# Last feed-forward chunk of a hybrid decoder layer: one bank state added from PSUM, and the closing LayerNorm's statistics, by VectorE; the scaling by ScalarE

## The chip, the cores and the metric

The kernel runs on one core of one Trainium2 chip. The metric is the device time of one execution in microseconds (us). The time before is the median of three runs, 904.08 us, between 903.46 and 904.77.

## The reference, cut to what matters

The layer is: a LayerNorm, a token mixer (gated linear attention and multi-head latent attention in parallel, gated and projected), a LayerNorm over the sum with the residual, a squared-ReLU feed-forward net, and the closing LayerNorm (LN2). All is float32, with 512 tokens and 1024 channels. What matters here is the end:

```
def layer_norm(x, g, b):
    mu = jnp.mean(xf, axis=-1, keepdims=True)
    var = jnp.mean(jnp.square(xf - mu), axis=-1, keepdims=True)
    return ((xf - mu) * lax.rsqrt(var + LN_EPS) * g + b).astype(x.dtype)
...
ff = jnp.square(jax.nn.relu(h @ w_ff1[l])) @ w_ff2[l]        # 512x1024 @ 1024x4096, @ 4096x1024
h = layer_norm(DEEPNORM_ALPHA * h + ff, ln2_g[l], ln2_b[l])
```

## The kernel before, in words

The 512 tokens are four tiles of 128 tokens (`tt` 0 to 3). `res[tt]` is a 128 x 1024 tile in SBUF with the residual (alpha times h, with LN1's weight and bias in it); the feed-forward result is added into it. Every float32 product is made of three matmuls over operands that are split into a high and a low part (`split`, lines 106 and 107, and `pump`, lines 180 and 181: ScalarE makes the high part, VectorE the low part).

The 4096 hidden channels are worked through in four chunks of 1024 (`ci` 0 to 3). In each chunk `gemm_fm` makes the hidden activations, and `win_f2` the second product, in Winograd's form of Strassen's scheme: seven block products ("phases" 0 to 6) over sums of token blocks, channel blocks and weight blocks. A phase has two halves, each one entry of the list `WIN`, and works on two token sub-tiles `t`. Phases 0, 3 and 6 accumulate in the same PSUM bank for each `t`, and so do phases 2 and 5; phase 1 and phase 4 have banks of their own. After the second half of a phase the bank's state is read out (lines 1160 to 1165): ScalarE copies it from PSUM into a tile `ev` (line 1163), and a DMA issued by GpSimd (POOL) adds it in SBUF to the halves of `res` that need it (line 1165). Columns 0 to 511 of a tile are its half `j` = 0, columns 512 to 1023 its half `j` = 1.

The last chunk (`end`) goes through the first eight entries (phases 0 to 3) in this way. The fourth state is that of phase 3: it is added to half 1 of tiles 0 and 1. The other three phases are then worked one sub-tile at a time by `tile_product`, and VectorE adds the bank straight to `res`: phase 5 to half 1 of tiles 0 and 1 (line 1182), phase 6 to both halves of tiles 2 and 3 (line 1189), phase 4 taken off half 0 of tile 2 (line 1192) and, in two pieces of 256 columns, of tile 3 (line 1200).

When a tile has its last term, `ln2(tt)` normalises it. Before the change there are three forms:

- Tile 0: VectorE makes the statistics (`bn_stats` on each half, line 1048, `bn_aggr`, line 1049), ScalarE adds epsilon and turns the mean's sign (lines 1050 and 1051).
- Tiles 1 and 2: ScalarE makes them, in two passes over 1024 columns that also give a sum (lines 1055 and 1056), and a small third instruction (line 1057).
- For tiles 0 to 2 POOL raises the variance to the power of -0.5 (line 1058), ScalarE makes `nmr` = -mean times that (line 1059) and normalises the tile (line 1060), VectorE multiplies by LN2's weight `gb[0]` (line 1061), and POOL issues a DMA that adds the tile to the output rows in DRAM (line 1062). Those rows were filled with LN2's bias beforehand by SyncE's (SP's) DMAs (line 1158).
- Tile 3: VectorE makes the statistics in four pieces of 256 columns (lines 1196 and 1201) and joins them (line 1065); epsilon (line 1066), POOL's power (line 1067), then VectorE subtracts the mean and multiplies by the weight in two halves (line 1070), multiplies by the power and adds the bias in two halves (line 1073), and SP stores each half (line 1074).

The order of the work in each engine's queue is set ahead of time by a planner with a cost model of its own; each queue then runs in that order, and an instruction that waits holds all behind it. `tc.issue_after(x)` keeps an instruction behind `x` in the planned order.

Of the kernel before, what the change touches and what calls it, by code (L numbers as in the profile page):

```python
# [10 lines left out]
F32 = mybir.dt.float32  # L11
# [4 lines left out]
AF = mybir.ActivationFunctionType  # L16
ALU = mybir.AluOpType
AX = mybir.AxisListType

P = 128  # L20
T = 512
D = 1024
NT = T // P
NK = D // P
LN_EPS = 1e-5
# [27 lines left out]
def tile_hybrid_block(ctx: ExitStack, tc: tile.TileContext, I, out, dbg=None):  # L53
    nc = tc.nc
# [10 lines left out]
    def nm(s):  # L65
        uid[0] += 1
        return f"{s}_{uid[0]}"
# [4 lines left out]
    def A(shape, dt=F32, n="a"):  # L72
        tag, bufs = ("C", 8) if n in TAG_C else (n, TAG_W[n]) if n in TAG_W else ("A", 24)
        return pa.tile(shape, dt, tag=tag, bufs=bufs, name=nm(n))

    def B(shape, dt=F32, n="b"):
        return pb.tile(shape, dt, tag="B", name=nm(n))

    def S(shape, dt=F32, n="s"):
        return sm.tile(shape, dt, tag=n, name=nm(n))  # L80
# [4 lines left out]
    def PX(shape=(P, T), dt=F32, n="px"):  # L85
        return px.tile(list(shape), dt, tag="px", name=nm(n))
# [4 lines left out]
    act = nc.scalar.activation  # L91
    vtt = nc.vector.tensor_tensor
    vts = nc.vector.tensor_scalar
    stt = nc.vector.scalar_tensor_tensor
    gtt = nc.gpsimd.tensor_tensor
    mm = nc.tensor.matmul

    def bcast_row(name):
        t = A([P, D], F32, "bc")
        src = I[name]  # L100
        nc.scalar.dma_start(t, bass.AP(tensor=src.tensor, offset=src.offset, ap=[[0, P], [1, D]]))
        return t
# [24 lines left out]
    mhalf = consts.tile([P, 8], F32, name="mhalf")  # L127
# [7 lines left out]
    st = {"dma": 0, "spl": 0, "gates": ()}  # L135
# [60 lines left out]
    def spawn(g):  # L196
        active.append(g)
        return g

    def step(g):  # L200
        try:
            next(g)
        except StopIteration:
            active.remove(g)
# [3 lines left out]
    def tick(width):  # L208
        for g in list(active[:width or WID[0]]):
            step(g)  # L210

    def finish(*gs):
        while any(g in active for g in gs):
            for g in list(active):
                if g in gs:
                    step(g)
# [113 lines left out]
    def win_items(ci):  # L330
        return WIN if ci < FC - 1 else WIN[:8] + WIN[10:12] + WIN[8:10] + WIN[12:]
# [421 lines left out]
    scale = HQ ** -0.5  # L753
# [205 lines left out]
    t0, mv = mla_pair(0)  # L959
    mv()  # L960
    y_gla(1)
    t1, mv = mla_pair(1)
    mv(lambda: finish(*t0))
    t2, mv = mla_pair(2)
    mv(lambda: finish(*t1))
    t3, mv = mla_pair(3)
    mv(lambda: finish(*t2))
    y_mla(0)
    res = []
# [66 lines left out]
            yield  # L1036


    def ln2(tt, bst=None):
        r = res[tt]  # L1040
        rows = out[tt * P:(tt + 1) * P, :]
        if tt < 3:
            mv, nmr = S([P, 2], F32, "mv"), S([P, 1], F32, "nmr")
            nmean, var = mv[:, 0:1], mv[:, 1:2]
            if tt == 0:
                bst = S([P, 2, 6], F32, "bst")
                for j in range(2):
                    nc.vector.bn_stats(bst[:, j, :], r[:, j * T:(j + 1) * T])
                nc.vector.bn_aggr(mv, bst)
                act(var, var, AF.Copy, bias=LN_EPS)  # L1050
                act(nmean, nmean, AF.Copy, scale=-1.0)
            else:

                j = A([P, D], F32, "junk")
                act(j, r, AF.Copy, scale=-1.0 / D, accum_out=nmean)
                act(j, r, AF.Square, bias=nmean, accum_out=var)
                act(var, var, AF.Copy, scale=1.0 / D, bias=LN_EPS)
            gtt(var, var, mhalf[:, 0:1], op=ALU.pow)
            act(nmr, nmean, AF.Copy, scale=var)
            act(r, r, AF.Identity, scale=var, bias=nmr)  # L1060
            vtt(r, r, gb[0], op=ALU.mult)
            nc.gpsimd.dma_start(rows, r, accum_op=ALU.add)
        else:
            mv = S([P, 2], F32, "mv")
            nc.vector.bn_aggr(mv, bst)
            vts(mv[:, 1:2], mv[:, 1:2], LN_EPS, None, op0=ALU.add)
            gtt(mv[:, 1:2], mv[:, 1:2], mhalf[:, 0:1], op=ALU.pow)
            for j in range(2):
                c = slice(j * T, (j + 1) * T)
                stt(r[:, c], r[:, c], mv[:, 0:1], gb[0][:, c], op0=ALU.subtract, op1=ALU.mult)  # L1070
            for j in range(2):
                c = slice(j * T, (j + 1) * T)
                stt(r[:, c], r[:, c], mv[:, 1:2], gb[1][:, c], op0=ALU.mult, op1=ALU.add)
                nc.sync.dma_start(rows[:, c], r[:, c])
        yield

    def win_load(ci):
        w2 = I["w_ff2"].rearrange("(k p) n -> p k n", p=P)
# [43 lines left out]
    def win_f2(ci, hid):  # L1122
        bank = {}
        end = ci == FC - 1
        items = win_items(ci)

        def product(n, pp, t, cols=slice(0, T), new=None):
            op, hf, ph = items[n]
            hi, lo = stream[PL["f2", ci][n]]["w"]
            key = ({3: 0, 6: 0, 5: 2}.get(ph, ph), t)  # L1130
            opens = key not in bank
            if opens:
                bank[key] = (PX if key[0] < 2 else MM)()
            o, c = bank[key], slice(t * P, (t + 1) * P)
            if new is not None:
                o, opens = new, hf == 0 and pp == 0
            while ph not in hid[2 * hf + pp]:
                tick(4)
            xh, xl = hid[2 * hf + pp][ph]
            mm(o, xh[:, c], hi[:, pp, cols], start=opens, stop=False, skip_group_check=True)  # L1140
            mm(o, xh[:, c], lo[:, pp, cols], start=False, stop=False, skip_group_check=True)  # L1141
            mm(o, xl[:, c], hi[:, pp, cols], start=False, stop=hf == 1 and pp == 1, skip_group_check=True)  # L1142
            return o

        for n, (op, hf, ph) in enumerate(items[:8] if end else items):
            pump(PL["f2", ci][n])
            for pp in range(2):
                for t in range(2):
                    product(n, pp, t)
                tick(4)  # L1150
            if n in (5, 6):
                t2, q21 = WT.pop((ci, n - 5))
                vtt(t2, t2, q21, op=ALU.subtract)
                WQ[ci, "T4", n - 5] = t2
            if end and n == 6:
                gb.extend([bcast_row("ln2_g"), bcast_row("ln2_b")])
                for tt in range(3):
                    nc.sync.dma_start(out[tt * P:(tt + 1) * P, :], gb[1])
            if hf == 1:
                for t in range(2):  # L1160
                    o = bank[{3: 0, 6: 0, 5: 2}.get(ph, ph), t]
                    e = B([P, T], F32, "ev")
                    st["ev"] = act(e, o, AF.Copy, scale=-1.0 if ph == 4 else 1.0)  # L1163
                    for tt, j in (((0, 0),), ((0, 0),), ((2, 1),), ((0, 1),), ((2, 0),), ((0, 1),), ((2, 0), (2, 1)))[ph]:
                        nc.gpsimd.dma_start(res[tt + t][:, j * T:(j + 1) * T], e, accum_op=ALU.add)  # L1165
            if n == 9 and not end:
                win_load(ci + 1)
        if not end:
            return

        pump(PL["f2", ci][13])

        def tile_product(ns, t, c0=0, w=T, new=None):
            for n in ns:
                for pp in range(2):
                    o = product(n, pp, t, slice(c0, c0 + w), new)
                    tick(4)
            return o

        for t in range(2):  # L1180
            o = tile_product((8, 9), t)
            vtt(res[t][:, T:], res[t][:, T:], o, op=ALU.add)
            spawn(ln2(t))
        bst = S([P, 4, 6], F32, "bst4")
        for t in range(2):
            r = res[2 + t]
            o = tile_product((12, 13), t)
            r2 = r.rearrange("p (j c) -> p j c", c=T)
            vtt(r2, r2, o[:, None, :].to_broadcast([P, 2, T]), op=ALU.add)
            if t == 0:  # L1190
                o = tile_product((10, 11), t)
                vtt(r[:, :T], r[:, :T], o, op=ALU.subtract)
                spawn(ln2(2))
                continue
            for j in range(2):
                nc.vector.bn_stats(bst[:, 2 + j, :], r[:, T + j * 256:T + (j + 1) * 256])
            for j in range(2):
                c = slice(j * 256, (j + 1) * 256)
                o = tile_product((10, 11), t, j * 256, 256, PX()[:, :256])
                vtt(r[:, c], r[:, c], o, op=ALU.subtract)  # L1200
                nc.vector.bn_stats(bst[:, j, :], r[:, c])
        finish(spawn(ln2(3, bst)))

    gb = []
    WQ, WT = {}, {}
# [81 lines left out]
```

## Time and profile before

| What | Value |
|---|---|
| median of three runs | 904.08 us (903.46 to 904.77) |
| profiled execution: span from the first to the last instruction | 901.4 us |
| mean granted TensorE clock of the span | 0.995 |
| TensorE matmul busy | 878.1 us, 97% of the span |
| VectorE busy | 566.1 us, 63% |
| ScalarE busy | 439.8 us, 49% |
| GpSimd busy | 172.8 us, 19% |

The page gives the span of the profiled execution and no time of its own beside that. The span is 2.7 us under the median of the runs; a difference between two spans is therefore read as the same difference between two times. In the rows PE is TensorE (matmuls), DVE is VectorE, ACT is ScalarE, POOL is GpSimd and SP is SyncE. A row of a timeline has the start in us from the span's start, the duration in us, the engine, the line of the kernel, the operation, and output<-input; brackets tell how long the engine had been idle before it and what released it. Successive instructions of one engine overlap by a little, so that starts lie closer together than durations. Rows with x2 cover two instructions. Matmul ends are modelled.

### The profile page before, as it was taken

Reading aid. Unit: us, or ns where it says so; the run is one execution under the profiler, and the core shown is the slowest. Engines: PE = TensorE matmul, PEld = TensorE weight load, DVE = VectorE, ACT = ScalarE, POOL = GpSimd, SP = SyncE. Lnnn points to the kernel's source line nnn. Section 1 sums busy time; section 2 is a strip of 40 time slices with the busy share of each in tenths; the row PEclk is TensorE's granted clock in tenths of the full one; section 3 lists DMA queues with packets and bytes.
Section 4 is the critical chain, followed back from the end, with each engine's and each line's share of the span. In section 5 each row is a group of like instructions: output and inputs, shape, how many; then the busy total and the mean of one; then the engine's idle time right before and its main releaser. Section 6 shows DMA issues by size and latency. Waiting matters only on the chain.

```text
span 901.4 us, 11728 instructions
## 1 busy us (share of the span) xinstructions
PE 878.1 (97%) x4472; PEld 746.5 (83%) x4472; DVE 566.1 (63%) x919; ACT 439.8 (49%) x745; POOL 172.8 (19%) x203
## 2 busy tenths in 40 slices
PE   5999999999999999999999999999999999999994
PEld 5988888888888888888888888988888888888883
DVE  7835855575635244657756797997557656754666
ACT  5555443444434333435645423366357546645654
POOL 1003442442511010000000002104400520241032
PEclk9999999999999999999999999999999999999997
DMA  7413213212213332212207618005940990397084
GB/s 243 122 47 94 90 52 94 71 47 71 75 38 93 88 105 74 68 42 65 94 24 260 205 49 303 2 0 139 302 120 25 261 249 25 80 312 169 1 210 94
DMA packets 63335, 101.47 MB, mean 113 GB/s; under 512 B 7680, under 2 KB 31616, under 8 KB 63280
## 3 DMA queue, kind: packets, MB, share of 16 engines
q1 hardware_dynamic: 48256, 64.04, 22.7%
q0 software_dynamic: 13104, 33.04, 15.2%
q10 hardware_dynamic: 1920, 3.66, 1.2%
q8 instruction: 35, 0.57, 0.3%
q14 instruction: 20, 0.16, 0.1%
HBM read 82.36 MB, written 3.67 MB: 95 GB/s over the span
## 4 chain that ended last, share of the span: by engine, by line
PE 92%; DMA 2%; ACT 2%; POOL 1%; issue 1%; DVE 1%; POOLq 0%; DVEq 0%; ACTq 0%
PE mm L231 16%; PE mm L233 15%; PE mm L232 15%; PE mm L264 6%; PE mm L265 6%; PE mm L266 6%; PE px L1141 3%; PE px L1140 3%; PE px L1142 3%; PE mm L1141 2%; PE mm L1140 2%; PE mm L1142 2%; PE px L680 2%; DMA res<-ev 1%; PE px L837 1%
## 5 line engine op out<-in xcount | busy, mean ns | idle before, releaser
L181 DVE TENSOR_TENSOR wlo<-wraw,whi 128x1024 fp32r<-128x1024 f32 (+1 forms) x104 | 117.7, 1132 | 162.3 <-ACT whi L180 154.9
L231 PE MATMUL mm<-h,whi 128*128 128x512 f32 x416 | 162.6, 392 | 0.4 <-ACT gt L924 0.4
L232 PE MATMUL mm<-h,whi 128*128 128x512 f32 x416 | 162.4, 390 | 0.0
L180 ACT ACTIVATE whi<-wraw 128x1024 fp32r<-128x1024 f32 (+1 forms) x104 | 100.3, 964 | 118.7 <-PE mm L232 68.3
L233 PE MATMUL mm<-h,wlo 128*128 128x512 f32 x416 | 154.9, 390 | 0.0
L1165 POOL DMA_DIRECT2D res<-ev x56 | 48.6, 980 | 238.2 <-ACT ev L1163 195.8
L231 PEld LDWEIGHTS mm<-h,whi 128*128 128x128 f32 x416 | 78.1, 188 | 16.3 <-ACT gt L924 0.6
L233 PEld LDWEIGHTS mm<-h,wlo 128*128 128x128 f32 x416 | 77.9, 188 | 16.4 <-DVE wlo L181 0.3
L232 PEld LDWEIGHTS mm<-h,whi 128*128 128x128 f32 x416 | 78.2, 188 | 15.6
L265 PE MATMUL mm<-wlo,h 128*128 128x512 f32 x128 | 50.3, 393 | 0.0
L266 PE MATMUL mm<-whi,h 128*128 128x512 f32 x128 | 50.1, 392 | 0.0
L264 PE MATMUL mm<-whi,h 128*128 128x512 f32 x128 | 49.7, 403 | 0.0
L1214 ACT ACTIVATE relu<-mm 128x512 f32<-128x512 f32 x32 | 18.8, 595 | 56.8 <-PE mm L233 56.8
L352 POOL TENSOR_TENSOR mv<-mv,mhalf 128x1 f32<-128x1 f32 x4 | 4.6, 1154 | 211.7 <-DVE mv L351 211.7
L619 POOL TENSOR_TENSOR rp<-rp 128x256 f32<-128x256 f32 x32 | 31.4, 983 | 60.9 <-ACT E L624 44.1
L626 DVE TENSOR_TENSOR M<-E,qk 128x512 f32<-128x512 f32 x32 | 27.3, 853 | 16.5 <-ACT E L624 16.5
L624 ACT ACTIVATE E<-rp 128x512 f32<-128x512 f32 x32 | 20.4, 638 | 26.9 <-POOL rp L620 26.9
L180 ACT ACTIVATE xh<-wraw 128x1024 fp32r<-128x1024 f32 (+1 forms) x20 | 19.0, 959 | 24.7 <-PE mm L266 16.0
L181 DVE TENSOR_TENSOR wlo<-wq,whi 128x1024 fp32r<-128x1024 f32 x15 | 18.4, 1223 | 19.7 <-ACT whi L180 19.7
L620 POOL TENSOR_TENSOR rp<-rp 128x256 f32<-128x256 f32 x32 | 27.5, 860 | 10.3 <-ACT q L649 8.1
L266 PEld LDWEIGHTS mm<-whi,h 128*128 128x128 f32 x128 | 24.0, 188 | 5.0
L265 PEld LDWEIGHTS mm<-wlo,h 128*128 128x128 f32 x128 | 24.1, 188 | 4.3
(383 smaller groups left out, 2240.9 us busy)
## 6 DMA issues: line engine op xcount, KB each, us to landing
wraw<-in_w_in_dram SPq DMA_DIRECT2D x40, 512.0 KB, 3.5
wraw<-in_w_ff_dram SPq DMA_DIRECT2D x32, 512.0 KB, 7.6
wq<-in_w_ff_dram POOLq DMA_DIRECT2D x32, 512.0 KB, 9.4
res<-ev POOLq DMA_DIRECT2D x56, 256.0 KB, 8.3
wraw<-in_w_o_gla_dram SPq DMA_DIRECT2D x8, 512.0 KB, 3.7
wraw<-in_w_o_mla_dram SPq DMA_DIRECT2D x8, 512.0 KB, 3.2
wraw<-in_w_out_dram SPq DMA_DIRECT2D x8, 512.0 KB, 4.3
wraw<-in_w_in_dram SPq DMA_DIRECT2D x8, 360.0 KB, 5.1
```

Source lines behind the costliest of these rows:

```text
L180: st["ins"] = act(hi[:, :nk, :n], raw[:, :nk, :n], AF.Copy)
L181: vtt(lo[:, :nk, :n], raw[:, :nk, :n], f(hi[:, :nk, :n]), op=ALU.subtract)
L231: mm(o, hi[:, c], xh, start=first, stop=False)
L232: mm(o, hi[:, c], xl, start=False, stop=False)
L233: mm(o, lo[:, c], xh, start=False, stop=last)
L264: mm(o, xh, hi[:, :n], start=opens, stop=False, skip_group_check=share)
L265: mm(o, xh, lo[:, :n], start=False, stop=False, skip_group_check=share)
L266: mm(o, xl, hi[:, :n], start=False, stop=last, skip_group_check=share)
L1140: mm(o, xh[:, c], hi[:, pp, cols], start=opens, stop=False, skip_group_check=True)
L1141: mm(o, xh[:, c], lo[:, pp, cols], start=False, stop=False, skip_group_check=True)
L1142: mm(o, xl[:, c], hi[:, pp, cols], start=False, stop=hf == 1 and pp == 1, skip_group_check=True)
L1165: nc.gpsimd.dma_start(res[tt + t][:, j * T:(j + 1) * T], e, accum_op=ALU.add)
```

## The change

It touches only the last chunk's end and `ln2`.

- The fourth state (phase 3) is no longer copied by ScalarE and added by two DMAs: VectorE adds it to half 1 of tiles 0 and 1 straight from PSUM (new line 1157).
- All statistics are VectorE's `bn_stats` (new function `ln2_stats`, line 1046) and `bn_aggr` (line 1053). Half 0 of tiles 0 and 1 is held behind those two additions in the planned order; the other halves follow the addition that completes them.
- For tiles 0 to 2, ScalarE adds epsilon (line 1055), POOL makes the power (line 1056), VectorE subtracts the mean and multiplies by the weight in one instruction (line 1057), ScalarE multiplies by the power (line 1058), and POOL issues the DMA that adds the tile to the output rows (line 1059).
- Tile 3 keeps its steps under new line numbers (1061 epsilon, 1062 power, 1065, 1068, 1069 store).
- `ln2` is no generator any more: it issues all its work where it is called.

```diff
-    def ln2(tt, bst=None):
+    LN2 = [None] * NT
+
+    def ln2_stats(tt, j, w=T, c0=0):
+        if LN2[tt] is None:
+            LN2[tt] = (S([P, 4 if tt == 3 else 2, 6], F32, f"bst{tt}"), S([P, 2], F32, "mv"))
+        c = j * T + c0
+        i = 2 * j + c0 // w if tt == 3 else j
+        nc.vector.bn_stats(LN2[tt][0][:, i, :], res[tt][:, c:c + w])
+
+    def ln2(tt):
...
         if tt < 3:
...
-                j = A([P, D], F32, "junk")
-                act(j, r, AF.Copy, scale=-1.0 / D, accum_out=nmean)
-                act(j, r, AF.Square, bias=nmean, accum_out=var)
-                act(var, var, AF.Copy, scale=1.0 / D, bias=LN_EPS)
-            gtt(var, var, mhalf[:, 0:1], op=ALU.pow)
-            act(nmr, nmean, AF.Copy, scale=var)
-            act(r, r, AF.Identity, scale=var, bias=nmr)
-            vtt(r, r, gb[0], op=ALU.mult)
+            act(rstd, rstd, AF.Copy, bias=LN_EPS)
+            gtt(rstd, rstd, mhalf[:, 0:1], op=ALU.pow)
+            stt(r, r, mean, gb[0], op0=ALU.subtract, op1=ALU.mult)
+            act(r, r, AF.Copy, scale=rstd)
             nc.gpsimd.dma_start(rows, r, accum_op=ALU.add)
...
                 for t in range(2):
                     o = bank[{3: 0, 6: 0, 5: 2}.get(ph, ph), t]
+                    if end and ph == 3:
+                        st["p6"] = vtt(res[t][:, T:], res[t][:, T:], o, op=ALU.add)
+                        continue
                     e = B([P, T], F32, "ev")
...
         for t in range(2):
+            with tc.issue_after(st["p6"].ins):
+                ln2_stats(t, 0)
+        for t in range(2):
             o = tile_product((8, 9), t)
             vtt(res[t][:, T:], res[t][:, T:], o, op=ALU.add)
-            spawn(ln2(t))
+            ln2_stats(t, 1)
+            ln2(t)
...
             if t == 0:
+                ln2_stats(2, 1)
                 o = tile_product((10, 11), t)
                 vtt(r[:, :T], r[:, :T], o, op=ALU.subtract)
-                spawn(ln2(2))
+                ln2_stats(2, 0)
+                ln2(2)
                 continue
             for j in range(2):
-                nc.vector.bn_stats(bst[:, 2 + j, :], r[:, T + j * 256:T + (j + 1) * 256])
+                ln2_stats(3, 1, 256, j * 256)
...
-        finish(spawn(ln2(3, bst)))
+        ln2(3)
```

In the planned order of the changed kernel TensorE's instructions stand in the same order as before. VectorE's queue at the end reads: the two additions from PSUM (1157), `bn_stats` of half 0 of tiles 0 and 1; then for tile 0 and for tile 1 the addition 1182, `bn_stats`, `bn_aggr`, the multiplication 1057; then for tile 2 the addition 1189, `bn_stats`, the subtraction 1193, `bn_stats`; then tile 3's addition 1189, tile 2's `bn_aggr`, two `bn_stats` of tile 3, tile 2's multiplication 1057, tile 3's two subtractions 1202, its last two `bn_stats`, `bn_aggr`, and the steps 1061, 1065 and 1068.

More of the change, by code (lines that the diff above doesn't have):

```diff
@@ L1036, in residual1 @@
             yield
-    def ln2(tt, bst=None):
+    LN2 = [None] * NT
[6 more added lines that the diff above has]
+    def ln2(tt):
         r = res[tt]
         rows = out[tt * P:(tt + 1) * P, :]
+        bst, mv = LN2[tt]
+        mean, rstd = mv[:, 0:1], mv[:, 1:2]
+        nc.vector.bn_aggr(mv, bst)
@@ L1042, in ln2 @@
         if tt < 3:
[L1043 to L1052, printed above, removed]
-                j = A([P, D], F32, "junk")
-                act(j, r, AF.Copy, scale=-1.0 / D, accum_out=nmean)
-                act(j, r, AF.Square, bias=nmean, accum_out=var)
-                act(var, var, AF.Copy, scale=1.0 / D, bias=LN_EPS)
@@ L1058, in ln2 @@
-            gtt(var, var, mhalf[:, 0:1], op=ALU.pow)
-            act(nmr, nmean, AF.Copy, scale=var)
[L1060 to L1074, printed above, removed]
@@ L1075, in ln2 @@
-        yield
+            act(rstd, rstd, AF.Copy, bias=LN_EPS)
+            gtt(rstd, rstd, mhalf[:, 0:1], op=ALU.pow)
+            stt(r, r, mean, gb[0], op0=ALU.subtract, op1=ALU.mult)
+            act(r, r, AF.Copy, scale=rstd)
+            nc.gpsimd.dma_start(rows, r, accum_op=ALU.add)
+            return
+        vts(rstd, rstd, LN_EPS, None, op0=ALU.add)
+        gtt(rstd, rstd, mhalf[:, 0:1], op=ALU.pow)
+        for j in range(2):
+            c = slice(j * T, (j + 1) * T)
+            stt(r[:, c], r[:, c], mean, gb[0][:, c], op0=ALU.subtract, op1=ALU.mult)
@@ L1077, in win_load @@
+        for j in range(2):
+            c = slice(j * T, (j + 1) * T)
+            stt(r[:, c], r[:, c], rstd, gb[1][:, c], op0=ALU.mult, op1=ALU.add)
+            nc.sync.dma_start(rows[:, c], r[:, c])
     def win_load(ci):
@@ L1180, in win_f2 @@
         for t in range(2):
+            with tc.issue_after(st["p6"].ins):
+                ln2_stats(t, 0)
+        for t in range(2):
             o = tile_product((8, 9), t)
             vtt(res[t][:, T:], res[t][:, T:], o, op=ALU.add)
-            spawn(ln2(t))
-        bst = S([P, 4, 6], F32, "bst4")
+            ln2_stats(t, 1)
+            ln2(t)
         for t in range(2):
@@ L1200, in win_f2 @@
                 vtt(r[:, c], r[:, c], o, op=ALU.subtract)
-                nc.vector.bn_stats(bst[:, j, :], r[:, c])
-        finish(spawn(ln2(3, bst)))
+                ln2_stats(3, 0, 256, j * 256)
+        ln2(3)
     gb = []
```

## The prediction

> **What bounds the kernel now.** I read the page first (shares), then the busy time by stretches of the last 30 us, the chain of waits, and the timelines of the engines there. The page says that TensorE is the bound:
>
> ```profile
> span 901.4 us, 11728 instructions
> PE 878.1 (97%) x4472; PEld 746.5 (83%) x4472; DVE 566.1 (63%) x919; ACT 439.8 (49%) x745; POOL 172.8 (19%) x203
> ```
>
> The change leaves TensorE's instructions in their order, so it can only gain or lose where TensorE is not the bound: after its last matmul. The stretches (busy us and count of PE, PEld, DVE, ACT, POOL, then granted clock, DMA share, GB/s) show that part:
>
> ```profile
> 878.70:888.50 9.80, 9.80 (x54) 8.40 (x52) 6.33 (x8) 6.54 (x13) 2.01 (x3) 1.00 0.29 46
> 888.50:893.58 5.08, 0.04 (x1) 0.00 (x0) 4.34 (x8) 3.12 (x6) 1.41 (x2) 0.88 0.38 52
> 893.58:901.40 7.82, 0.00 (x0) 0.00 (x0) 3.15 (x7) 0.00 (x0) 1.78 (x2) 0.50 0.81 178
> ```
>
> TensorE is done at 888.5 and 12.9 us follow: 5.1 us until VectorE joins tile 3's statistics (893.58), and 7.8 us from there to the end. The chain of waits (start, length, what) tells what fills the time before 893.58:
>
> ```profile
> 872.52 6.16 DMA res<-ev
> ...
> 887.62 1.13 ACT res L1060
> 888.75 1.14 ACT junk L1056 x2
> ...
> 891.17 1.25 ACT res L1060
> 892.44 1.23 DVE res L1061
> ```
>
> The fourth state's DMA lands at 878.68; only then can VectorE finish tile 0. From there ScalarE has statistics, `nmr` and normalisation of tiles 0 to 2 in one queue; its last pass, over tile 2, ends at 892.42, and VectorE must multiply that tile ahead of tile 3's `bn_aggr`. So ScalarE's queue, not TensorE, sets 893.58.
>
> **The change, part by part.** The terms come from VectorE's timeline (start, duration):
>
> ```profile
> 871.10 1.22 DVE L181 TENSOR_TENSOR xl<-wq,xh 128x1024 fp32r<-128x1024 f32 x1
> 878.77 0.69 DVE L1182 TENSOR_TENSOR res<-res,mm 128x512 f32<-128x512 f32 x1 [6.46 <-DMA res<-ev]
> 879.50 0.69 DVE L1048 BATCH_NORM_STATS2 bst<-res 128x6 f32<-128x512 f32 x1
> 880.23 0.21 DVE L1049 BATCH_NORM_AGGREGATE mv<-bst 128x2 f32<-128x12 f32 x1
> ...
> 884.16 1.21 DVE L1189 TENSOR_TENSOR res<-res,px 128x1024 f32<-128x1024 f32 x1
> 885.47 0.69 DVE L1192 TENSOR_TENSOR res<-res,mm 128x512 f32<-128x512 f32 x1
> ...
> 889.92 0.75 DVE L1196 BATCH_NORM_STATS2 bst<-res 128x6 f32<-128x256 f32 x2
> 890.59 0.73 DVE L1200 TENSOR_TENSOR res<-res,px 128x256 f32<-128x256 f32 x2
> 891.24 0.75 DVE L1201 BATCH_NORM_STATS2 bst<-res 128x6 f32<-128x256 f32 x2
> 892.44 1.23 DVE L1061 TENSOR_TENSOR res<-res,bc 128x1024 f32<-128x1024 f32 x1 [0.45 <-ACT res L1060]
> 893.58 0.26 DVE L1065 BATCH_NORM_AGGREGATE mv<-bst 128x2 f32<-128x24 f32 x1
> ...
> 893.94 1.40 DVE L1070 SCALAR_TENSOR_TENSOR res<-res,mv,bc 128x512 f32<-128x512 f32 x2
> 895.78 1.41 DVE L1073 SCALAR_TENSOR_TENSOR res<-res,mv,bc 128x512 f32<-128x512 f32 x2 [0.43 <-POOL mv L1067]
> ```
>
> and from TensorE's, the last matmul of each product that VectorE waits for (duration modelled):
>
> ```profile
> 875.77 0.39 PE L1142 MATMUL mm<-xh,xl 128*128 128x512 f32 x1
> ...
> 878.49 0.39 PE L1142 MATMUL mm<-xh,xl 128*128 128x512 f32 x1
> ...
> 882.80 0.39 PE L1142 MATMUL mm<-xh,a 128*128 128x512 f32 x1
> ...
> 885.52 0.39 PE L1142 MATMUL px<-xh,xl 128*128 128x512 f32 x1
> ...
> 888.26 0.28 PE L1142 MATMUL px<-xh,a 128*128 128x256 f32 x1
> ```
>
> *The fourth state.* Two copies by ScalarE and two DMAs on POOL's queue go; two additions 128x512 from PSUM come on VectorE, 0.69 each like line 1182, which reads PSUM too. VectorE's last split ends at 872.3 and it then idles 6.46 us, so they run until about 873.7, and half 0's two `bn_stats` (0.69 each) until about 875.1. That is before 876.16, when tile 0's product is ready: hidden. If that idle time were gone they would cost 4 x 0.69 = 2.8 us in VectorE's queue. TensorE writes this bank again only with phase 6, long after. The second `bn_stats` waits for an accumulating DMA of phase 1, issued at 866.9, with VectorE's whole queue behind it; its landing:
>
> ```profile
> res<-ev POOLq DMA_DIRECT2D x1, 256.0 KB, 5.1
> ```
>
> 866.9 + 5.1 = 872.0: not late. The removed DMAs only lighten the traffic; no other queue loses or gains an instruction ahead of these.
>
> *Tiles 0 to 2 on VectorE.* New are two `bn_stats` and one `bn_aggr` for each of tiles 1 and 2, and the multiplication 1061 becomes the longer 1057. Its form stands elsewhere in the profile, at 1282 ns against 1225:
>
> ```profile
> L988 DVE SCALAR_TENSOR_TENSOR res<-res,mvin,bc 128x1024 f32<-128x1024 f32 x4 | 4.9, 1282 | 0.0
> L1056 ACT ACTIVATE junk<-res,mv 128x1024 f32<-128x1024 f32 x2 | 2.3, 1143 | 0.0
> ```
>
> I lay the queue out with 0.04 us between dependent instructions. Tile 0: 876.2, then 0.69 + 0.69 + 0.21 + 1.28: until 879.2. Tile 1 the same (its product is ready at 878.88): until 882.1. Tile 2: 1189 (1.21), `bn_stats`, 1193 (the product is ready at 883.19), `bn_stats`: until 885.25. Tile 3's product is ready at 885.52 + 0.39 = 885.91, so VectorE waits again, 0.66 us: everything added so far is hidden beside TensorE. From 885.95 nothing waits for TensorE but the two subtractions, ready since 888.54:
>
> - 1189 of tile 3, 1.21: to 887.16; tile 2's `bn_aggr` and two `bn_stats`, from 887.21, 0.67 from start to start of the next: 887.88.
> - 1057 of tile 2, 1.28 less 0.08 overlap: 889.08. The subtractions 0.65 (890.59 to 891.24): 889.73. Two `bn_stats` 0.75 and 0.04: `bn_aggr` at 890.52.
>
> Before, `bn_aggr` stood at 893.58: 3.06 us earlier. In these terms VectorE carries tile 2 and the wait on ScalarE is gone.
>
> *The rest of the tail.* From `bn_aggr` tile 3's steps are the same: 0.36 to line 1070, 1.84 to line 1073, 5.62 to the end of the span, 7.82 in all. What must hold is POOL's power, ready 0.4 after both instructions of line 1070. POOL's rows:
>
> ```profile
> 885.68 0.56 POOL L1058 TENSOR_TENSOR mv<-mv,mhalf 128x1 f32<-128x1 f32 x1 [0.26 <-ACT mv L1057]
> 890.26 0.55 POOL L1058 TENSOR_TENSOR mv<-mv,mhalf 128x1 f32<-128x1 f32 x1 [4.01 <-ACT mv L1057]
> ...
> 893.97 0.85 POOL L1062 DMA_DIRECT2D out_dram<-res  x1 [2.30 <-DVE mv L1065]
> 894.53 1.21 POOL L1067 TENSOR_TENSOR mv<-mv,mhalf 128x1 f32<-128x1 f32 x1
> ```
>
> The power takes 0.56 beside VectorE's instructions that have one input in SBUF (a PSUM addition, `bn_stats`) and 1.21 beside line 1070, which reads two SBUF tensors, whose end (895.34) it seems to await. I take 1.21 again. Bounds: at 0.56 the wait of 0.43 goes (gain 3.5); and where tile 2's power runs first (ready at about 887.6 to 888.2) it may hold line 1057, due at 887.88, by 0.3 (gain 2.8).
>
> The Trainium skill, page "SBUF — State Buffer", section "Who interferes with whom", says that a VectorE instruction with two SBUF inputs contends with a GpSimd instruction that reads SBUF, and that the first to issue blocks the other fully. The trace agrees in the direction that it shows (1.21 against 0.56); a power that holds VectorE it does not show here. By the rule the sum would be 2.8 us of gain, without any such lock 3.5.
>
> *Tile 2's store.* ScalarE's scaling has one pointer operand, like line 1056: 1.14. From 889.16 it ends at 890.35, POOL issues then, and the store lands 5.1 later:
>
> ```profile
> out_dram<-res POOLq DMA_DIRECT2D x3, 512.0 KB, 5.1
> ...
> out_dram<-res SPq DMA_DIRECT2D x2, 256.0 KB, 3.1
> ...
> 896.56 0.99 SPq L1074 DMA_DIRECT2D out_dram<-res  x2
> ```
>
> That is 895.5, ahead of tile 3's halves, issued 0.78 and about 1.4 (the second piece of line 1073 and one more of these issues) behind line 1073 at 892.72 and landing at 896.6 to 897.3. POOL's issue stands ahead of the last power in its queue, as now. The last stores meet less traffic (tile 1's store is out by about 888, now it is issued at 890.79); I take no gain for that, at most 0.4, the spread of landings.
>
> **Sum.** -3.06, rounded -3.1 us: the span 901.4 becomes 898.3, and the median 904.08, which is 2.7 above this span, becomes 901.0. Ends: -2.8 and -3.5 - 0.4 = -3.9 (901.3 and 900.2).
>
> **Rivals.**
> - *The power holds line 1057* (the lower bound): 901.3. For it: the times overlap in my layout by 0.3; against: VectorE may reach 1057 first.
> - *The gain is larger*: the last power is not held, the stores land sooner: 900.2 to 900.6. Against: the only row of that power is 1.21.
> - *A new wait in VectorE's queue eats it.* Tile 1's `bn_stats` of half 0 stands ahead of everything for LN2 and waits for the DMA of phase 1. Behind it VectorE has 14.6 us of work until `bn_aggr` (the instructions listed above). If that DMA lands at 878.7, when the last accumulation lands now, `bn_aggr` is at 893.3 and the time 903.8: no change. *Slower* begins where it lands later than 879.0; at 881 the time is 906.1. Against: its landing is read at 872.0, and the DMAs that shared its time are fewer now.
> - *The change doesn't do what it says*: ScalarE's scaling and tile 2's store set the end instead. They are 1.1 us ahead of the last store, so it takes a landing of over 6.2 us to count, and over 9.3 to cancel the gain: not likely; it counts under no change.
>
> **Chances.** The forecast 0.5, the power in the way 0.16, the larger gain 0.12; no change 0.13 (half of it the new wait, half the store, or TensorE's own stretch of 888 us shifting by 1 us from one build to the next); slower 0.09 (the new wait, or such a shift with little gain). A measurement can tell 0.2%, 1.8 us, from no change: faster is below 902.3. So faster 0.78, same 0.13, slower 0.09. The likeliest case has 900.5 to 901.5; the range takes in the bounds on both sides, half a microsecond of scatter of a median (the runs lie 1.3 apart), and the nearer part of "no change": 899.8 to 902.8.
>
> **What would show it.** Right: no DMA from `ev` after phase 2; VectorE's two PSUM additions at about 872; VectorE waiting for TensorE, not ScalarE, at 885.9; `bn_aggr` of tile 3 about 2 us after TensorE's last matmul, with line 1057 at 1.28; line 1068 still waiting 0.4 for a power of 1.2. Wrong: VectorE's idle time ahead of tile 0's addition ends with a DMA; ScalarE's last scaling or tile 2's store lies on the chain's end; TensorE's last matmul lies elsewhere than 888.5.

## The result, and the profile after

The changed kernel takes 900.46 us (median of five runs, 900.14 to 901.28) beside 903.77 us before: 3.3 us less, a ratio of 0.9962 with a 95% interval of 0.995 to 0.9974. The forecast was 901.0; it started from 904.08, the median of the first three runs of the kernel before, and over all five that median is 903.77. Measured again in the second set of experiments it was 900.23 beside 903.34 (0.9967, 0.9954 to 0.9979).

The page of the changed kernel begins:

```profile
span 898.7 us, 11716 instructions
PE 878.0 (98%) x4472; PEld 746.2 (83%) x4472; DVE 570.2 (63%) x927; ACT 432.7 (48%) x731; POOL 172.8 (19%) x201
```

TensorE does the same work; VectorE has 4 us more of it, ScalarE 7 us less, and the span is 2.7 us shorter. TensorE's last matmul comes 0.22 us later in this execution than in that of before:

```profile
888.48 0.28 PE L1136 MATMUL px<-xh,a 128*128 128x256 f32 x1
```

Over all profiled kernels here it starts between 887.77 and 888.98, so spans are compared below by their distance from it. VectorE's timeline after the change:

```profile
871.87 1.27 DVE L1157 TENSOR_TENSOR res<-res,px 128x512 f32<-128x512 f32 x2
873.06 1.28 DVE L1046 BATCH_NORM_STATS2 bst<-res 128x6 f32<-128x512 f32 x2
876.42 0.69 DVE L1182 TENSOR_TENSOR res<-res,mm 128x512 f32<-128x512 f32 x1 [2.08 <-PE mm L1136]
...
886.17 1.22 DVE L1189 TENSOR_TENSOR res<-res,px 128x1024 f32<-128x1024 f32 x1 [0.70 <-PE px L1136]
...
888.09 1.27 DVE L1057 SCALAR_TENSOR_TENSOR res<-res,mv,bc 128x1024 f32<-128x1024 f32 x1
...
890.72 0.27 DVE L1053 BATCH_NORM_AGGREGATE mv<-bst 128x2 f32<-128x24 f32 x1
...
892.92 1.41 DVE L1068 SCALAR_TENSOR_TENSOR res<-res,mv,bc 128x512 f32<-128x512 f32 x2 [0.43 <-POOL mv L1062]
```

The fourth state is in `res` at 873.1 instead of 878.7, half 0's statistics follow at once, and both of VectorE's waits before TensorE's end are now for TensorE. No wait for ScalarE is left. Tile 3's `bn_aggr` stands 2.24 us behind the start of the last matmul (890.72 - 888.48), where it stood 5.32 behind (893.58 - 888.26). The end of the chain of waits:

```profile
886.17 1.22 DVE res L1189
...
888.18 1.20 DVE res L1057
...
889.44 1.16 ACT res L1058
...
890.89 0.34 POOL out_dram L1059
...
891.29 1.61 POOLq L1285
...
892.92 0.75 DVE res L1068
```

The last step on VectorE waits for the power, and the chain leads from there not to VectorE's own statistics but over POOL's issue of tile 2's store back to ScalarE's scaling and VectorE's multiplication of tile 2. It ends with VectorE's queue and does not show what the stores wait for; the DMA queues do, below.

All kernels of the study, with the distances (us) from the start of the last matmul to tile 3's `bn_aggr`, to VectorE's last step (the multiplication by the power, its first half), to POOL's issue of tile 2's store and to the end of the span, and the time that this store takes from issue to landing. "Gain" is the median against that of before in the same set.

| Kernel | Median | Gain | Ratio, 95% interval | `bn_aggr` | last step | store issued | landing | end |
|---|---|---|---|---|---|---|---|---|
| before | 903.77 | | | 5.32 | 7.52 | 5.71 | 5.1 | 13.14 |
| changed | 900.46 | 3.3 | 0.995 to 0.9974 | 2.24 | 4.44 | 2.41 | 5.4 | 10.22 |
| e1, fourth state alone | 902.13 | 1.6 | 0.9975 to 0.9992 | 3.23 | 5.43 | 3.62 | 5.6 | 11.61 |
| e2, statistics alone | 901.86 | 1.9 | 0.9971 to 0.9989 | 4.14 | 6.34 | 4.31 | 5.3 | 11.93 |
| e3, scaling first | 901.66 | 2.1 | 0.9972 to 0.9989 | 1.44 | 4.27 | 3.99 | 5.1 | 11.50 |
| e4, weight in PSUM | 900.66 | 3.1 | 0.9953 to 0.998 | 2.24 | 3.92 | 2.41 | 5.2 | 10.03 |
| e5, changed again | 900.23 | 3.1 | 0.9954 to 0.9979 | 2.24 | 4.44 | 2.42 | 5.1 | 9.81 |
| e6, tile 2 ahead | 898.20 | 5.1 | 0.9929 to 0.9956 | 1.81 | 3.50 | 0.44 | 5.1 | 8.11 |
| e7, e6 by halves | 898.80 | 4.5 | 0.9939 to 0.9964 | 1.81 | 3.38 | 0.45 | 5.0 | 8.72 |
| e8, no store of tile 2 | 898.75 | 4.6 | 0.9936 to 0.9963 | 2.25 | 3.94 | | | 8.51 |

e1 to e4 ran beside each other (before: 903.73), e5 to e8 likewise (before: 903.34).

The last columns show what the end follows. In the seven kernels from before to e5 the end lies 2.3 to 2.4 us behind the landing of tile 2's store (store issued + landing), while its distance from VectorE's last step goes from 5.4 to 7.2. Tile 3's stores, which SP issues, have to wait for it. The DMA queues of the changed kernel (packets, MB, their time as a share of 16 engines; q0 holds what POOL issues, q1 what SP issues), first from SP's first issue on, 893.70 to 895.40, then from 895.40 to 897.40:

```profile
q0 software_dynamic: 82, 0.34, 103.9%
...
q1 hardware_dynamic: 288, 0.52, 68.8%
q0 software_dynamic: 21, 0.02, 6.3%
```

For 1.70 us only tile 2's packets move, and tile 3's start when few of these are left. In e8, which has no store of tile 2, they start 0.8 us behind their issue (892.80), and all of them move between 893.60 and 895.60:

```profile
q1 hardware_dynamic: 288, 0.52, 70.6%
```

So in the kernel before and in the changed one alike, tile 2's store sets the end, and VectorE's last step does not. The step came 3.1 us nearer to the last matmul, the landing of the store 3.0 (5.71 + 5.1 against 2.41 + 5.4), the end 2.9. Only in e6, e7 and e8 is that store early enough or missing.

### The profile page after: what moved, and what is told of

Read it like the earlier page. It is cut to its first block, busy times and chain, and to the rows that moved or that the text cites. A ratio compares the mean times of both kernels' runs of the same rounds, so it can differ in the third digit from the quotient of the medians.

```text
span 898.7 us, 11716 instructions
## 1 busy us (share of the span) xinstructions
PE 878.0 (98%) x4472; PEld 746.2 (83%) x4472; DVE 570.2 (63%) x927; ACT 432.7 (48%) x731; POOL 172.8 (19%) x201
## 4 chain that ended last, share of the span: by engine, by line
PE 96%; ACT 1%; DVE 1%; POOL 1%; DMA 1%; issue 0%; POOLq 0%; SPq 0%; DVEq 0%; ACTq 0%
PE mm L231 16%; PE mm L233 15%; PE mm L232 15%; PE mm L264 6%; PE mm L266 6%; PE mm L265 6%; PE px L1134 3%; PE px L1135 3%; PE px L1136 3%; PE mm L1134 2%; PE mm L1135 2%; PE mm L1136 2%; PE px L680 2%; PE px L837 1%; PE px L266 1%; PE px L264 1%
## 5 line engine op out<-in xcount | busy, mean ns | idle before, releaser
L1162 POOL DMA_DIRECT2D res<-ev x54 | 46.8, 978 | 240.1 <-ACT ev L1160 192.0
```

## The experiments

**e1: the fourth state alone.** The kernel before, with one edit:

```diff
+                    if end and ph == 3:
+                        vtt(res[t][:, T:], res[t][:, T:], o, op=ALU.add)
+                        continue
                     e = B([P, T], F32, "ev")
```

> Only the fourth state is added by VectorE from PSUM; statistics, normalisation and multiplication stay as before. My theory (ScalarE's queue of statistics and normalisations set the end, and it was started late by the DMA of the fourth state): tile 0's addition starts at about 876.2 in place of 878.8, ScalarE's last normalisation (tile 2) ends at about 890.0 in place of 892.4, VectorE's multiplication of tile 2 goes at once after tile 3's bn_stats, and bn_aggr of tile 3 stands at about 891.6 in place of 893.6: 2.0 us faster than before (901.8), so this part alone gives over half of the gain. Rival (the statistics' move is the whole gain, the DMA was hidden in the end because tile 2 is late anyway): within 0.5 us of before.

Measured: 1.6 us faster than before, where 2.0 was expected, and the rows that the theory named (VectorE, then ScalarE, then the last matmul):

```profile
890.78 1.23 DVE L1061 TENSOR_TENSOR res<-res,bc 128x1024 f32<-128x1024 f32 x1
891.92 0.26 DVE L1065 BATCH_NORM_AGGREGATE mv<-bst 128x2 f32<-128x24 f32 x1
...
889.51 1.24 ACT L1060 ACTIVATE res<-res,nmr,mv 128x1024 f32<-128x1024 f32 x1
...
888.69 0.28 PE L1142 MATMUL px<-xh,a 128*128 128x256 f32 x1
```

ScalarE's last normalisation ends at 890.75, just in time for VectorE's multiplication, which now hardly waits. `bn_aggr` is 2.1 us earlier against the last matmul (5.32 to 3.23), the 2.0 of the theory; tile 2's store is issued as much earlier, but took 5.6 us to land in this execution instead of 5.1, and the end came 1.5 nearer. Half of the whole gain in time comes with it. The DMA was not hidden.

**e2: the statistics alone.** The changed kernel without the branch of e1: the fourth state goes through ScalarE's copy and two DMAs again, and half 0's statistics stand behind those copies.

> Statistics by VectorE and the new order of multiplication and scaling, but the fourth state still copied by ScalarE and added by DMA. My theory: VectorE waits for that DMA until about 878.8 and then has an unbroken queue; tile 3's addition starts at about 887.8 in place of 886.0, bn_aggr at about 892.4: 1.2 us faster than before (902.6), 2.1 us slower than the changed kernel. The two parts' gains then overlap: 2.0 + 1.2 is near 3.3, but each alone leaves another queue at the end. Rival (the statistics' move is the whole gain): as fast as the changed kernel, 900.5.

```profile
878.41 0.69 DVE L1179 TENSOR_TENSOR res<-res,mm 128x512 f32<-128x512 f32 x1 [4.84 <-PE mm L1136]
...
887.37 1.20 DVE L1186 TENSOR_TENSOR res<-res,px 128x1024 f32<-128x1024 f32 x1
...
891.91 0.26 DVE L1053 BATCH_NORM_AGGREGATE mv<-bst 128x2 f32<-128x24 f32 x1
...
887.77 0.28 PE L1136 MATMUL px<-xh,a 128*128 128x256 f32 x1
```

VectorE starts tile 0 at 878.41. The row names TensorE, but that product was done some 2.7 us earlier (it ended at 876.16 before, and this execution's matmuls stand 0.49 earlier); what came last must be the fourth state's DMA, the other thing that the addition needs (inferred: this row doesn't name it). From there VectorE's queue has no gap: tile 3's addition starts at 887.37 behind it, without a wait, and `bn_aggr` is 1.2 us earlier against the last matmul than before (5.32 to 4.14), as forecast. The time fell by 1.9, and the 1.2 expected lies in the interval's reach (1.0 to 2.6). This kernel also has a wait that the changed one has not: tile 1's `bn_stats` of half 0 stands ahead of VectorE's last split here and waits 1.06 for phase 1's DMA, until 871.76; TensorE was not late by it. So each part alone gives about half, each through another queue: in e1 VectorE and ScalarE together, in e2 VectorE started late. Together they give 3.3, near the sum of 1.6 and 1.9; in the distance of the end from the last matmul it is 1.5 and 1.2 alone, and 2.9 and 3.3 together (changed, e5).

**e3: scaling first.** The changed kernel with the third part undone for tiles 0 to 2:

```diff
+            nmr = S([P, 1], F32, "nmr")
...
+            act(mean, mean, AF.Copy, scale=-1.0)
             gtt(rstd, rstd, mhalf[:, 0:1], op=ALU.pow)
-            stt(r, r, mean, gb[0], op0=ALU.subtract, op1=ALU.mult)
-            act(r, r, AF.Copy, scale=rstd)
+            act(nmr, mean, AF.Copy, scale=rstd)
+            act(r, r, AF.Identity, scale=rstd, bias=nmr)
+            vtt(r, r, gb[0], op=ALU.mult)
```

> As the changed kernel, but for tiles 0 to 2 ScalarE normalises (scale and nmr) and VectorE multiplies by the weight afterwards, as tile 0 before. My theory: VectorE's work is the same in length, and in the planned order tile 2's multiplication stands between the two halves of tile 3's subtraction, so it waits for ScalarE no more than a few tenths; bn_aggr of tile 3 about 1.2 us earlier than in the changed kernel, its last step (the multiplication by the power) about 0.5 earlier, tile 2's store 0.9 later: 900.0 to 900.6, no difference that counts. The merged multiplication would then give nothing by itself. Rival (merging is what takes the wait for ScalarE out of VectorE's queue): 1 us slower than the changed kernel, 901.5.

The time is the rival's (901.66, 1.2 us less gain than the changed kernel), the way is not. From its timeline, VectorE's rows and POOL's issue of tile 2's store:

```profile
891.27 1.22 DVE L1061 TENSOR_TENSOR res<-res,bc 128x1024 f32<-128x1024 f32 x1
...
893.07 1.41 DVE L1071 SCALAR_TENSOR_TENSOR res<-res,mv,bc 128x512 f32<-128x512 f32 x2
...
892.79 0.87 POOL L1062 DMA_DIRECT2D out_dram<-res  x1 [1.03 <-DVE res L1061]
```

and from its DMA issues (count, size of each, median us from issue to landing):

```profile
out_dram<-res SPq DMA_DIRECT2D x2, 256.0 KB, 4.7
```

VectorE does not wait for ScalarE, and its last step is 0.17 us nearer to the last matmul than in the changed kernel, as my theory had it (`bn_aggr` is 0.8 earlier, where it had 1.2). But tile 2's multiplication comes late in the queue, its store is issued 1.6 us later against the last matmul (3.99 behind it, 2.41 in the changed kernel), and tile 3's stores, issued about 1 us behind it, take 4.7 us to land where the changed kernel's take about 3. They land right behind it again: the end is 2.4 behind tile 2's landing, as in the changed kernel. My theory had left that out; e6 and e8 measure it.

**e4: tile 3's weight read from PSUM.**

```diff
+    LNP = []
...
-            stt(r[:, c], r[:, c], mean, gb[0][:, c], op0=ALU.subtract, op1=ALU.mult)
+            stt(r[:, c], r[:, c], mean, LNP[0][:, :T], op0=ALU.subtract, op1=ALU.mult)
...
+        LNP.append(bank[0, 0])
```

> As the changed kernel, but tile 3's subtraction multiplies by a bank that lies in PSUM in place of LN2's weight in SBUF: the output of tile 3 is not the reference's. Theory (the last power of POOL is held by VectorE's instruction with two SBUF inputs): the power takes about 0.6 in place of 1.4 and VectorE's last step no longer waits 0.43 for it: 0.4 us faster than the changed kernel. Rival (the power is late because POOL has just issued tile 2's store): the power still takes over 1 us and the wait stays.

```profile
891.28 0.88 POOL L1060 DMA_DIRECT2D out_dram<-res  x1 [2.43 <-ACT res L1059]
891.89 0.85 POOL L1063 TENSOR_TENSOR mv<-mv,mhalf 128x1 f32<-128x1 f32 x1
...
892.79 1.41 DVE L1069 SCALAR_TENSOR_TENSOR res<-res,mv,bc 128x512 f32<-128x512 f32 x2
```

The power takes 0.85 instead of 1.39 (the 0.6 expected is that of a power that doesn't stand behind an issue of POOL's), ends before VectorE's two subtractions do, and the wait of 0.43 is gone: the last step is 0.52 us nearer to the last matmul. So VectorE's instruction with two SBUF inputs does hold the power. Yet the time did not fall (900.66 beside 900.46 and 900.23). Tile 2's store is issued where it was, 2.41 behind the last matmul, and the end followed it, not VectorE's step: tile 3's stores, issued half a microsecond earlier, took about as much longer to land (3.2 and 2.9 in the two executions of the changed kernel):

```profile
out_dram<-res SPq DMA_DIRECT2D x2, 256.0 KB, 3.6
```

**e5 to e8.** e5 is the changed kernel once more. e6 puts tile 2's `bn_aggr` and multiplication ahead of tile 3's addition:

```diff
-            stt(r, r, mean, gb[0], op0=ALU.subtract, op1=ALU.mult)
+            st["mul"] = stt(r, r, mean, gb[0], op0=ALU.subtract, op1=ALU.mult)
...
-            vtt(r2, r2, o[:, None, :].to_broadcast([P, 2, T]), op=ALU.add)
+            with tc.issue_after(st["mul"].ins):
+                vtt(r2, r2, o[:, None, :].to_broadcast([P, 2, T]), op=ALU.add)
```

e7 adds to e6 that tile 3's last two steps go half by half (`issue_after` holds half 1's subtraction behind half 0's last step). e8 is the changed kernel without tile 2's store.

> The changed kernel once more, beside the three others of this set: 3.0 to 3.5 us faster than before, by every theory.

> As the changed kernel, but tile 2's bn_aggr and multiplication stand ahead of tile 3's addition in VectorE's queue, in the 0.7 us in which it waits for TensorE there. Theory A (the last steps of VectorE and tile 2's store both set the end): bn_aggr and the last step 0.4 us earlier, tile 2's store issued 2.0 us earlier (at about 888.9), its traffic out of the way of tile 3's two stores, which land in 2.7 to 3.1 us; 0.5 to 0.9 us faster than the changed kernel. Theory B (only VectorE's last step sets the end): 0.4 us faster.

> As the previous kernel, and tile 3's last two steps go half by half: subtraction and power of half 0, then of half 1. The power is then held by one instruction of 0.74 instead of two: half 0's last step starts 0.65 us earlier, half 1's ends 0.1 earlier. Theory A and B: 0.1 to 0.3 us faster than the previous kernel, since the last store is that of half 1.

> As the changed kernel, with tile 2's store left out (its output rows hold the bias alone). Theory A (its traffic delays tile 3's stores): VectorE's last step where it is, tile 3's stores landing in about 2.7 us in place of 3.2, 0.3 to 0.6 us faster than the changed kernel. Theory B: the same time.

In e5 and e6 the last matmul starts at the same 888.19, so their rows can be set side by side. First e5's timeline (VectorE, POOL) and its DMA issues:

```profile
890.43 0.26 DVE L1053 BATCH_NORM_AGGREGATE mv<-bst 128x2 f32<-128x24 f32 x1
...
890.80 1.40 DVE L1065 SCALAR_TENSOR_TENSOR res<-res,mv,bc 128x512 f32<-128x512 f32 x2
892.63 1.42 DVE L1068 SCALAR_TENSOR_TENSOR res<-res,mv,bc 128x512 f32<-128x512 f32 x2 [0.43 <-POOL mv L1062]
...
890.61 0.88 POOL L1059 DMA_DIRECT2D out_dram<-res  x1 [2.44 <-ACT res L1058]
891.22 1.38 POOL L1062 TENSOR_TENSOR mv<-mv,mhalf 128x1 f32<-128x1 f32 x1
```

```profile
out_dram<-res SPq DMA_DIRECT2D x2, 256.0 KB, 2.9
```

Then the same of e6:

```profile
885.45 1.28 DVE L1057 SCALAR_TENSOR_TENSOR res<-res,mv,bc 128x1024 f32<-128x1024 f32 x1
...
890.00 0.27 DVE L1053 BATCH_NORM_AGGREGATE mv<-bst 128x2 f32<-128x24 f32 x1
...
890.37 1.41 DVE L1065 SCALAR_TENSOR_TENSOR res<-res,mv,bc 128x512 f32<-128x512 f32 x2
891.69 1.41 DVE L1068 SCALAR_TENSOR_TENSOR res<-res,mv,bc 128x512 f32<-128x512 f32 x2
...
888.63 0.88 POOL L1059 DMA_DIRECT2D out_dram<-res  x1 [1.48 <-ACT res L1058]
890.61 0.92 POOL L1062 TENSOR_TENSOR mv<-mv,mhalf 128x1 f32<-128x1 f32 x1 [1.10 <-DVE mv L1061]
```

```profile
out_dram<-res SPq DMA_DIRECT2D x2, 256.0 KB, 2.1
```

e6 is 2.0 us faster than e5 (898.20 against 900.23), more than theory A's 0.9. Three things add up in the rows: `bn_aggr` 0.43 earlier; the wait for the power gone, another 0.51 (892.63 to 891.69 is 0.94 in all); and the stores landing 0.8 sooner. By e4, earlier steps on VectorE count only because the store's issue moved too, from 2.42 to 0.44 behind the last matmul. The second was not in the theory. With tile 2's store issued 2.0 us earlier POOL is free when the variance is ready. The power then ends at 891.53, 0.42 behind the first of VectorE's two subtractions (891.11) and before the second one ends. In e5, behind POOL's issue, it ends at 892.60, 0.40 behind the second (892.20). That it awaits the one that is running when it begins is argued, not shown: e5's row of the power starts at 891.22, inside the first subtraction as well, and the account holds if it really begins where POOL's issue ends, at 891.49, by when the second is under way (from about 891.46).

e8 leaves VectorE's work and `bn_aggr` where they were and takes only tile 2's store away. Tile 3's subtractions and POOL's power in its timeline, and the landing among its DMA issues:

```profile
890.70 1.40 DVE L1066 SCALAR_TENSOR_TENSOR res<-res,mv,bc 128x512 f32<-128x512 f32 x2
...
890.93 0.92 POOL L1063 TENSOR_TENSOR mv<-mv,mhalf 128x1 f32<-128x1 f32 x1 [2.86 <-DVE mv L1062]
```

```profile
out_dram<-res SPq DMA_DIRECT2D x2, 256.0 KB, 2.1
```

It is 1.5 us faster than e5: the last step 0.50 nearer to the last matmul, the landings 0.8 shorter. That is theory A, and more than its 0.6, because the step moved too, which A had left where it was. Theory B, only VectorE's last step sets the end, falls: 0.50 of the step is not 1.5, and e4 gave the same step without the time.

e7 is 0.6 us slower than e6, where 0.1 to 0.3 faster was expected:

```profile
892.36 0.75 DVE L1067 SCALAR_TENSOR_TENSOR res<-res,mv,bc 128x512 f32<-128x512 f32 x1 [0.46 <-POOL mv L1062]
893.03 0.74 DVE L1066 SCALAR_TENSOR_TENSOR res<-res,mv,bc 128x512 f32<-128x512 f32 x1
893.81 0.75 DVE L1067 SCALAR_TENSOR_TENSOR res<-res,mv,bc 128x512 f32<-128x512 f32 x1
```

The expectation rested on the wait of 0.43, which e6 had already removed, and here VectorE's last step does set the end. In halves VectorE has nothing to do while half 0's power is made and waits 0.46 again; the last half ends 5.58 us behind the last matmul (893.81 + 0.75 - 888.98) against 4.91 in e6.

## Why the prediction was right

- **What bounds the kernel.** Right up to `bn_aggr`, wrong behind it (see tile 2's store). The DMA of the fourth state and ScalarE's queue set 893.58: undoing either alone leaves about half of the gain (e1, e2).
- **The fourth state's cost on VectorE.** Right: 1.27 and 1.28 in time that was idle, followed by 2.08 us of waiting for TensorE. The accumulating DMA that the second `bn_stats` waits for was not late (in e2 VectorE's wait for it ended 5.2 us behind its issue at 866.55; 5.1 was taken), so the rival "a new wait in VectorE's queue" did not come.
- **VectorE's queue.** Right to some hundredths. Forecast: a free 0.66 before tile 3's addition, and `bn_aggr` 2.26 behind the last matmul (890.52 - 888.26). Measured: 0.70 and 2.24. Line 1057 took 1.27 to 1.28, forecast 1.28. In part that is luck: from tile 3's addition to tile 2's `bn_aggr` 1.26 was taken and 1.13 came, and from there to line 1057 0.67 was taken, with nothing for the `bn_aggr` itself, and 0.79 came.
- **The last power.** The wait of 0.43 came as taken; the power's row has 1.39, taken was 1.21. The reason given was half of it. The prediction had the power await both subtractions; in e6 and e8, where POOL is free when the variance is ready, it awaits only the first, so it met the second because POOL was issuing tile 2's store.
- **The rival "the power holds line 1057".** Did not happen. POOL's rows of the changed kernel, for tiles 0 and 2:

```profile
878.46 1.36 POOL L1056 TENSOR_TENSOR mv<-mv,mhalf 128x1 f32<-128x1 f32 x1 [5.42 <-ACT mv L1055]
...
887.90 0.56 POOL L1056 TENSOR_TENSOR mv<-mv,mhalf 128x1 f32<-128x1 f32 x1 [2.76 <-ACT mv L1055]
```

Tile 2's power runs from 887.90 to 888.46; line 1057 starts at 888.09 beside it and takes its usual 1.27. Tile 0's power, which came while line 1057 was running (until 879.39), took 1.36 and ended 0.43 behind it.

- **Tile 2's store.** Here a step failed, without harm to the sum. The prediction said that it lies 1.1 us ahead of the last store and needs a landing of over 6.2 us to count. It counts at its usual landing of 5.1 to 5.4: through the queue of POOL, and because tile 3's stores wait behind it, so that it sets the end. The 3.1 that the prediction took for the landing of those stores is about 2.1 of their own (e6, e8) and a wait of 1.0. Its rival "ScalarE's scaling and tile 2's store set the end instead" is what happened, before the change as well, and one of its signs of being wrong came: both stand on the chain's end (889.44 and 890.89). Without the store the changed kernel would be 1.5 us faster (e8). The forecast difference still held because two things moved by nearly the same: VectorE's last step, on which the sum was built, by 3.1, and the store's landing by 3.0 (3.3 in e5). The prediction gave no reason why they should, and e3 and e4 are kernels in which they do not; so far the sum was lucky. The tail from the last step to the end of the span was taken as unchanged at 5.62 and measured 5.78 and 5.37 in two executions, in which this store took 5.4 and 5.1 to land.
- **The upper bound.** It allowed 0.4 for stores that land sooner, "the spread of landings". No row that it shows has that spread; in e6 and e8 they land 0.8 sooner than in e5.
- **The sum.** 3.1 forecast, 3.3 and 3.1 measured.

## What to carry to other kernels

Where an engine's queue sets the end behind the last matmul, lay out each queue from the last product that it waits for; instruction durations of one profile gave the new end of VectorE's queue to a few hundredths here. Then look at the DMA queues as well: the chain of waits ended with VectorE's last step, while the end followed the store of the tile ahead. Moving work to an engine that has slack beside TensorE paid here because it ended before the last product did, and the late start (a DMA here) had to go together with the long queue, since either alone kept half the loss. The order at the end is worth as much as the work: putting the next-to-last tile's multiplication ahead of the last tile's addition, in part in a gap of 0.7 us and with no work saved, gave a further 2.0 us, mostly since its store left the way of both the last power and the last stores; that version (e6, 898.20 us) beats both kernels.

## What the runs showed of the hardware that was not expected

- *POOL's small instruction against VectorE's with two SBUF inputs.* The power alone takes 0.56; started on a free POOL during such an instruction it ends 0.40 to 0.43 behind that one instruction's end, also when the next of the kind follows at once (e6: the first subtraction ends at 891.11, the power at 891.53, the second at about 891.78). Reading one input from PSUM removes the hold (e4). In the other direction nothing was held (line 1057 beside tile 2's power, 1.27). The Trainium skill, page "SBUF — State Buffer", section "Who interferes with whom", has the first to issue block the other fully; the rows agree where VectorE was first and disagree where POOL was first.
- *A last store waits for the store ahead of it.* The two 256 KB stores of tile 3 landed in 2.0 to 2.1 us (median) with tile 2's 512 KB accumulating store left out or issued 3.7 to 3.8 us ahead (e8, e7, e6), in 2.9 to 3.7 with it issued 2.6 to 2.8 us ahead (before, changed, e1, e2, e5), in 3.6 with it 2.3 ahead (e4), and in 4.7 with it about 1 us ahead (e3). The extra time is a wait: none of their packets moved until tile 2's were nearly done, though SP issues the ones and POOL the other. The Trainium skill, page "DMA: Bandwidth & Descriptors", section "Latency and other measured facts", says that a lighter load on HBM makes the fixed cost of a transfer smaller; the runs show this wait instead, and do not tell whether that cost changed too, nor whether HBM or the shared DMA engines cause the wait.
- *TensorE's stretch ahead of the tail is not a constant.* With the same matmuls in the same order its last one started between 887.77 and 888.98 in ten profiled executions, a spread as large as some of the effects studied. It arises early: the 500th matmul starts between 104.9 and 106.1, and from it to the last all ten take 782.9 to 783.0 us. What causes it was not tried.
